# Weight splits on GpSimd in halves, one buffer more and other small moves in a hybrid decoder layer

## Chip, cores and metric

The kernel runs on one core of a Trainium2 chip. The metric is the device time of one execution in microseconds (us). A core has TensorE (PE in the profile; PEld is its loading of weights), VectorE (DVE), ScalarE (ACT), GpSimd (POOL) and SyncE (SP), which here only issues transfers.

## What is computed

One decoder layer in float32, with 512 tokens and a model width of 1024. A combined projection of the input feeds three token mixers; each is gated, projected back, gated again, and the merged result goes through an output projection and a LayerNorm.

```python
u = x @ w_in + b_in
a_x, a_z, b_q, b_k, b_v, b_z, i_q, i_k, i_w, c_q, c_kc, c_vc, c_ks, c_vs, c_kw, c_vw, c_g, c_z, g = split(u)
y_a = pool_mixer(a_x) * silu(a_z)
y_b = dsa_mixer(b_q, b_k, b_v, i_q, i_k, i_w) * silu(b_z)
y_c = nsa_mixer(c_q, c_kc, c_vc, c_ks, c_vs, c_kw, c_vw, c_g) * silu(c_z)
g = sigmoid(g)
m = g[0] * (y_a @ w_pa) + g[1] * (y_b @ w_pb) + g[2] * (y_c @ w_pc)
out = layernorm(ALPHA * x + m @ w_o)
```

The pool mixer takes trailing means over 2, 4, 8 and 16 tokens. The second mixer keeps the best keys of each query by an indexer's score. The third has a compressed, a selected and a window branch. The tests' inputs have larger spreads than usual for some weights; shapes are unchanged.

## The kernel before, in words

**Products in three parts.** Float32 accuracy comes from splitting each operand into a high and a low part: ScalarE rounds a copy into the high part (`h`), and the low part (`l`) is the original minus `h`. `mm3` (L67) then issues three matmuls of 512 columns: high by high, high by low and low by high (L68 to L70).

**Dense tiles.** The projection's weights are cut into 55 tiles of 128 outputs (128 x 1024 values, 512 KB). `dense` (L142) makes one tile in eight steps of three matmuls, into a PSUM buffer of the pool `pd` (three buffers) or `pq` (four). `load_w` (L87) brings a tile: a transfer into one of two staging buffers (`wst`), ScalarE's copy to `w_h` (L93), and the subtraction to `w_l` (L95). While `POOL[0]` is set, GpSimd issues the transfer and subtracts; at the start and the end SyncE and VectorE do. Smaller tiles of 512 columns (`wp`) serve the projections back (`branch_d`, L608).

**Opening.** Eight matmuls on a zeroed tile `idle` run while the first data come. `load_early` (L118) brings the first two weight tiles (numbers 0 and 3, `w0` and `w3`) in two halves each, `load_x` (L112) brings the input in eight pieces of 128 rows of the transpose (256 KB). The string in L129 gives their order: a and b are the first halves of the two weight tiles, c and d the second. L734 deals the steps of the first two dense tiles out in turns.

**Order of work.** TensorE's order is written out by hand: a stream `F` of generators (L742) is advanced a few steps between the pieces of the attention units (L809). The instructions of the other engines are placed by a planner from dependences, priorities and its own estimates of durations; instructions that are emitted under `high_priority` go ahead of others. Within an engine the order is then fixed.

**Attention units.** `Unit.front` (L423) makes scores (L443), adds a mask and takes the maximum on VectorE (L445), exponentials on ScalarE (L450), then the reciprocal and its scaling by a gate, `r` (L454 to L458), and probabilities `pc` or `pb` in two float16 parts: ScalarE L462, VectorE L464. The score's PSUM buffer is free after L464. `Compressed.probs` (L511) does the same for the compressed branch; its low part `cp` is made on VectorE in L524. Top-k rounds on VectorE (L305, L306) fill gaps.

**Small buffers.** The tag `b` has six buffers of 2 KB a partition. They hold gates (`z` in `silu2`, L403; `tg`), the pooling tiles (`x0`, the running sums `xs` that GpSimd adds in L569, and `za`), and a few constants. `silu2` reads a dense tile's PSUM twice on ScalarE, `tanh` (L407) and a biased copy into `z` (L153); then the PSUM buffer is free. `th`, `vc32` and `vc1` of the compression (L351, L384) are in another pool.

**Output projection.** `wo_mm` (L876) makes 512 x 512 in four row tiles for each half of the columns. For the first half the kernel takes seven of the eight steps of two tiles before the eighth of either (L891), because the last parts of the merged result (`mh`, `ml`) come late. `add_x` (L883) reads the PSUM on VectorE (L885) and frees it.

Of the kernel before, what the change touches and what calls it, by code (L numbers as in the profile page):

```python
# [7 lines left out]
F32 = mybir.dt.float32  # L8
F32R = mybir.dt.float32r
BF = mybir.dt.bfloat16  # L10
# [9 lines left out]
KT = D // 128  # L20
# [10 lines left out]
EARLY = (0, I_KK)  # L31
# [3 lines left out]
def trunk(ctx, tc, a, out, dbg=None):  # L35
    nc = tc.nc
# [4 lines left out]
    sp = ctx.enter_context(tc.tile_pool(name="sp", bufs=2))  # L41
# [1 line left out]
    pq = ctx.enter_context(tc.tile_pool(name="pq", bufs=4, space=PSUM))  # L43
    pv = ctx.enter_context(tc.tile_pool(name="pv", bufs=1, space=PSUM))

    BUFS = {"x": 8, "wst": 2, "wh": 3, "wl": 3, "s": 2, "p": 2, "pt": 2, "t": 16, "ks": 2, "b": 6}

    def big(tag, name, dt=F32, shape=(128, 2, 512)):
        return bp.tile(list(shape), dt, tag=tag, name=name, bufs=BUFS[tag])

    def sm(name, n=8, bufs=4):
        return sp.tile([128, n], F32, tag=name, name=name, bufs=bufs)

    def dps(name):
        return pd.tile([128, 512], F32, tag="pd", name=name)

    def qps(name):
        return pq.tile([128, 512], F32, tag="pq", name=name)

    def f(ap):  # L60
        return ap.bitcast(F32)

    def split(h, l, src):
        nc.scalar.activation(h, src, AF.Copy)
        nc.vector.tensor_sub(l, src, f(h))  # L65

    def mm3(ps, wh, wl, rh, rl, start, stop):  # L67
        nc.tensor.matmul(ps, wh, rh, start=start, stop=False)  # L68
        nc.tensor.matmul(ps, wh, rl, start=False, stop=False)  # L69
        nc.tensor.matmul(ps, wl, rh, start=False, stop=stop)  # L70
# [14 lines left out]
    POOL = [False]  # L85

    def load_w(src, n, tag="w"):  # L87
        st = big("wst", f"{tag}_st", F32, (128, 1024))[:, :n]
        h = big("wh", f"{tag}_h", F32R, (128, 1024))
        l = big("wl", f"{tag}_l", F32R, (128, 1024))  # L90
        with tc.high_priority():
            (nc.gpsimd if POOL[0] else nc.sync).dma_start(st, src)  # L92
            nc.scalar.activation(h[:, :n], st, AF.Copy)  # L93
            eng = nc.gpsimd if POOL[0] else nc.vector
            eng.tensor_sub(l[:, :n], st, f(h[:, :n]))  # L95
        return h, l


    idle = big("b", "idle", BF, (128, 512))
    nc.vector.memset(idle, 0.0)  # L100
    ps = qps("idle")
    for _ in range(8):
        nc.tensor.matmul(ps, idle[:, :128], idle, start=True, stop=True)


# [6 lines left out]
    def load_x(k):  # L112
        st = xst[k // 4][:, k % 4]
        dma = nc.sync.dma_start(st, a["xT"][:, k, :])
        split(xh[k // 2][:, k % 2, :], xl[k // 2][:, k % 2, :], st)
        return dma

    def load_early(i, c, n):  # L118
        if i not in early:
            early[i] = [big(t, f"w{i}{c}", d, (128, 1024)) for t, c, d in (  # L120
                ("s", "s", F32), ("t", "h", F32R), ("t", "l", F32R))]
        s = slice(c * 1024 // n, (c + 1) * 1024 // n)
        st, h, l = early[i]
        nc.sync.dma_start(st[:, s], a["wt"][i][:, s])
        split(h[:, s], l[:, s], st[:, s])

    bias = const("bias")
    with tc.high_priority():
        for k in "a01b23c4d567":  # L129
            if k in "abcd":  # L130
                load_early(EARLY["abcd".index(k) % 2], "abcd".index(k) // 2, 2)
            else:
                dma = load_x(int(k))
    ctx.enter_context(tc.issue_after(dma.ins))

    def X(part, k, s0=0, s1=S):
# [5 lines left out]
    def dense(i, s0=0, ps=None):  # L142
        wh, wl = early[i][1:] if i in early else load_w(a["wt"][i], 1024, f"w{i}")
        ps = (ps or dps)(f"d{i}")
        n = S - s0
        for k in range(KT):
            w = slice(k * 128, k * 128 + 128)
            mm3(ps[:, :n], wh[:, w], wl[:, w], X(0, k, s0), X(1, k, s0), k == 0, k == KT - 1)
            yield
        return ps[:, :n], bias[:, i:i + 1]  # L150
# [200 lines left out]
    def compress_mid(nm):  # L351
        w1h, w1l, bh, bl = CP[nm]
        ps = dps("cp" + nm)[:64, :62]
        for l in range(16):
            mm3(ps, w1h[:, l, :], w1l[:, l, :], bh[:, :, l], bl[:, :, l], l == 0, l == 15)
            if l % 4 == 3:
                yield
        th = sp.tile([64, 62], F32, name="th", bufs=1)
        nc.scalar.activation(th, ps, AF.Tanh, scale=0.5)
        z = big("b", "hz", F32, (64, 2, 4, 32))  # L360
        nc.vector.memset(z, 0.0)
        for g in range(2):
            c = slice(31 * g, 31 * g + 31)
            nc.vector.scalar_tensor_tensor(z[:, g, :, :31], th[:, None, c].to_broadcast([64, 4, 31]), 1.0,
                                           ps[:, None, c].to_broadcast([64, 4, 31]), op0=OP.add, op1=OP.mult)
        zh = big("b", "hth", F32R, (64, 2, 4, 32))
        zl = big("b", "htl", F32R, (64, 2, 4, 32))
        split(zh, zl, z)
        CP[nm] = zh, zl
# [13 lines left out]

    def compress_v():  # L384
        HH, HL, w2h, w2l = CP["v"] + W2[1]
        v32 = sp.tile([128, 2, 64], F32, name="vc32", bufs=1)
        ps = dps("vc")[:, :128].rearrange("p (g d) -> p g d", g=2)
        for g in range(2):
            mm3(ps[:, g], HH[:, g].rearrange("p r n -> p (r n)"), HL[:, g].rearrange("p r n -> p (r n)"),
                w2h, w2l, True, True)  # L390
        nc.vector.tensor_scalar(v32, ps, vscale, 0.5, op0=OP.mult, op1=OP.mult)
        for p in range(3):
            v1 = sp.tile([128, 2, 64], BF, name="vc1", bufs=2)
            nc.vector.tensor_copy(v1, v32)
            if p < 2:
                nc.vector.tensor_sub(v32, v32, v1)
            for h in range(4):
                r = slice(32 * h, 32 * h + 32)
                nc.gpsimd.tensor_copy(VC[p][r, :, h], v1[r])
        yield  # L400
# [207 lines left out]
    def branch_d(d, br, Y, t, dst):  # L608
        wh, wl = load_w(a["wp"][br, d], 512, f"wp{br}")
        ps = dps("pp")  # L610
        for e in range(4):
            w = slice(e * 128, e * 128 + 128)
            yh, yl = Y[e // 2]
            mm3(ps, wh[:, w], wl[:, w], yh[:, e % 2], yl[:, e % 2], e == 0, e == 3)
            yield
        with tc.high_priority():
            nc.vector.scalar_tensor_tensor(dst, t, 1.0, ps, op0=OP.add, op1=OP.mult)  # L617
# [113 lines left out]
    W2 = [compress_w2("k", 128), compress_w2("v", 64)]  # L731
    st = Stream([(dsa_keys,)])
    st2 = Stream([(f_kk, 0)])
    for n in (2, 1, 1, 1, 1, 1, 2):  # L734
        for _ in range(n):
            st.step()
        for _ in range(n):
            st2.step()
    Stream([(index_queries, 0), (f_qc, 0, 0), (values_load,), (index_queries, 1), (f_qc, 0, 1), (values,)]).rest()
    mcmp, rowv = small["mcmp"].rearrange("p (j n) -> p j n", j=NT), small["rowv"]  # L740
    POOL[0] = True
    F = Stream([(compress_in, I_KC, "k"), (vscales,), (compress_in, I_VC, "v"), (f_zc, 0, 0), (compress_mid, "k"),  # L742
                (f_zc, 0, 1), (compress_k,), (compress_mid, "v"), (f_qc, 1, 0), (f_qc, 1, 1), (compress_v,),
                (early_g, 0, 0), (f_kk, 1), (early_g, 0, 1), (f_pool,), (f_zc, 1, 0), (pool_x, 0), (early_g, 0, 2),
                (pool_z, 0), (pool_x, 1), (early_g, 0, 3), (pool_y, 0), (pool_z, 1), (pool_x, 2), (pool_y, 1),
# [130 lines left out]
    def wo_mm(ps, hf, t, k0, k1, c0=0, c1=512):  # L876
        c = slice(t * 128, (t + 1) * 128)
        for k in range(k0, k1):
            wh, wl = WO[hf][k // 2]
            mm3(ps[:, :c1 - c0], MH[k // 4][:, k % 4, c], ML[k // 2][:, k % 2, c], wh[:, k % 2, c0:c1],  # L880
                wl[:, k % 2, c0:c1], k == 0, k == KT - 1)

    def add_x(t, ps, c0, c1):  # L883
        z = Zt[t][:, c0:c1]
        nc.vector.scalar_tensor_tensor(z, ps[:, :c1 - c0], 0.5, z, op0=OP.mult, op1=OP.add)  # L885

    def stats(t, c0, c1):
        nc.vector.bn_stats(bst[t][:, c0 // 256 * 6:c0 // 256 * 6 + 6], Zt[t][:, c0:c1])

    bst = [sm("bst", 24) for _ in range(NT)]  # L890
    pss = [dps("wo"), dps("wo")]  # L891
    for k0, k1 in ((0, KT - 1), (KT - 1, KT)):
        for t in range(2):
            wo_mm(pss[t], 0, t, k0, k1)
    for t in range(NT):
        if t > 1:
            pss.append(dps("wo"))
            wo_mm(pss[t], 0, t, 0, KT)
        add_x(t, pss[t], 0, 512)
        for c in (0, 256):  # L900
            stats(t, c, c + 256)
    for t in range(NT):
# [17 lines left out]
        if not last:  # L920
            c = cs.pop()
# [81 lines left out]
```

## Time and profile before

| | |
|---|---|
| median of 3 runs | 529.67 us (529.11 to 530.96) |
| profiled execution | 529.6 us, of which the span from first to last instruction is 527.8 us |
| busy: TensorE, VectorE, ScalarE, GpSimd | 508.5, 378.7, 281.5, 219.8 us |
| mean granted TensorE clock | 0.991 of full speed |

The page gives busy time of each engine; matmuls are pipelined, so TensorE's busy time says that work is in flight and not that it runs at its peak. The list of waits says for which instruction of which engine an engine idled. A timeline row has the start, the duration, the engine, the line, the operation, output and inputs, and in brackets the engine's idle time just before and what ended it; "x2" means that two equal instructions in a row were merged.

### The profile page before, as it was taken

How to read it: one execution, taken by the hardware profiler on the slowest of the kernel's cores; microseconds unless marked ns; L12 is line 12 of the kernel's file. 1: busy time of each engine (PE TensorE's matmuls, PEld its weight loads, DVE VectorE, ACT ScalarE, POOL GpSimd, SP SyncE). 2: the span in 40 equal slices, each digit the busy share in tenths (PEclk: the TensorE clock that was granted, in tenths of full speed). 3: DMA queues.
4: the chain of work that ended last, by engine and by line, in shares of the span. 5: the costliest groups of instructions: out<-in, count | busy, mean ns of one | idle time of the engine just before them, and what ended most of it. 6: DMA issues, size and time to landing. Idle time of an engine off the chain costs nothing. (4 is left out here: it accounts for less than half of the span.)

```text
span 527.8 us, 7784 instructions
## 1 busy us (share of the span) xinstructions
PE 508.5 (96%) x2718; PEld 420.1 (80%) x2718; DVE 378.7 (72%) x912; ACT 281.5 (53%) x585; POOL 219.8 (42%) x205
## 2 busy tenths in 40 slices
PE   8999999988999999899999999999999999999993
PEld 5889878876888888688888788888788888887883
DVE  5773799789868798999787897956654345444276
ACT  6684475756566666673755647566663344432000
POOL 1424443463556467344544344427662112115042
PEclk9999999999999999899999999999999999999997
DMA  8622332168845342556534434453584445462012
GB/s 289 261 80 81 110 130 61 46 117 137 170 111 162 86 126 52 119 133 170 142 101 122 139 110 105 134 120 106 145 169 121 140 139 180 159 215 105 1 70 90
DMA packets 82135, 66.72 MB, mean 126 GB/s; under 512 B 67184, under 2 KB 68656, under 8 KB 82096
## 3 DMA queue, kind: packets, MB, share of 16 engines
q1 hardware_dynamic: 74912, 40.54, 28.9%
q0 software_dynamic: 7184, 25.69, 16.4%
q8 instruction: 21, 0.34, 0.3%
q14 instruction: 18, 0.15, 0.1%
HBM read 47.87 MB, written 2.10 MB: 95 GB/s over the span
## 5 line engine op out<-in xcount | busy, mean ns | idle before, releaser
L68 PE MATMUL d<-xh,w_h 128*128 128x512 f32 (+1 forms) x424 | 167.1, 394 | 2.6 <-ACT z L153 2.4
L69 PE MATMUL d<-xl,w_h 128*128 128x512 f32 (+1 forms) x424 | 165.2, 390 | 0.0
L70 PE MATMUL d<-xh,w_l 128*128 128x512 f32 (+1 forms) x424 | 165.1, 389 | 0.0
L95 POOL TENSOR_TENSOR w_l<-w_st,w_h 128x1024 fp32r<-128x1024 f32 x41 | 98.0, 2393 | 111.0 <-ACT w_h L93 109.9
L68 PEld LDWEIGHTS d<-xh,w_h 128*128 128x128 f32 x424 | 80.0, 189 | 18.5 <-ACT z L153 2.9
L70 PEld LDWEIGHTS d<-xh,w_l 128*128 128x128 f32 x424 | 79.9, 188 | 16.8
L69 PEld LDWEIGHTS d<-xl,w_h 128*128 128x128 f32 x424 | 79.9, 189 | 13.9
L93 ACT ACTIVATE w_h<-w_st 128x1024 fp32r<-128x1024 f32 x53 | 56.1, 1058 | 35.1 <-DMA w_st<-in_wt_dram 27.8
L450 ACT ACTIVATE qkc<-qkc,nb 128x512 f32<-128x512 f32 (+3 forms) x64 | 32.0, 500 | 51.2 <-DVE nb L445 32.5
L95 POOL TENSOR_TENSOR wp_l<-wp_st,wp_h 128x512 fp32r<-128x512 f32 x16 | 20.8, 1297 | 49.4 <-ACT wp_h L93 49.4
L464 DVE SCALAR_TENSOR_TENSOR pc<-qkc,r,pc 128x512 f16<-128x512 f32 (+3 forms) x64 | 32.7, 545 | 10.8 <-ACT pc L462 10.6
L643 POOL TENSOR_TENSOR m<-m,tg 128x512 f32<-128x512 f32 x12 | 16.5, 1377 | 52.8 <-DVE tg L617 52.6
L462 ACT ACTIVATE pc<-qkc,r 128x512 f16<-128x512 f32 (+3 forms) x64 | 29.8, 526 | 14.6 <-issue 7.1
L445 DVE CUSTOM_DVE_ANT_0 qkc<-qkc,cmask 128x512 f32<-128x512 f32 (+3 forms) x64 | 31.2, 495 | 2.7 <-PE qkc L443 2.3
L92 POOL DMA_DIRECT2D w_st<-in_wt_dram x41 | 23.3, 569 | 9.9 <-POOL w_l L95 5.3
L70 PE MATMUL wo<-woh,ml 128*128 128x512 f32 (+1 forms) x72 | 26.4, 367 | 0.4 <-DVE ml L65 0.4
L69 PE MATMUL wo<-wol,mh 128*128 128x512 f32 (+1 forms) x72 | 26.3, 366 | 0.0
L68 PE MATMUL wo<-woh,mh 128*128 128x512 f32 (+1 forms) x72 | 26.3, 366 | 0.0
L306 DVE MATCH_REPLACE8 acc<-m,acc 128x256 f32<-128x256 f32 (+2 forms) x48 | 26.0, 543 | 0.0
L95 DVE TENSOR_TENSOR w_l<-w_st,w_h 128x1024 fp32r<-128x1024 f32 x12 | 15.8, 1323 | 13.4 <-ACT w_h L93 13.4
L450 ACT ACTIVATE qkb<-qkb,nb 128x128 f32<-128x128 f32 (+3 forms) x32 | 16.0, 500 | 17.6 <-DVE nb L445 17.3
L305 DVE MAX8 m<-acc 128x8 f32<-128x256 f32 (+2 forms) x48 | 25.3, 549 | 0.0
(249 smaller groups left out, 1029.2 us busy)
## 6 DMA issues: line engine op xcount, KB each, us to landing
w_st<-in_wt_dram POOLq DMA_DIRECT2D x41, 512.0 KB, 3.8
w_st<-in_wt_dram SPq DMA_DIRECT2D x12, 512.0 KB, 3.8
wp_st<-in_wp_dram POOLq DMA_DIRECT2D x16, 256.0 KB, 3.0
wo_st<-in_wo_dram SPq DMA_DIRECT2D x8, 512.0 KB, 3.6
xst<-in_xT_dram SPq DMA_DIRECT2D x8, 256.0 KB, 4.7
wp_st<-in_wp_dram SPq DMA_DIRECT2D x8, 256.0 KB, 2.7
z<-in_x_dram SPq DMA_DIRECT2D x4, 512.0 KB, 5.0
wvst<-in_wve_dram SPq DMA_DIRECT2D x4, 320.0 KB, 7.1
```

Source lines behind the costliest of these rows:

```text
L68: nc.tensor.matmul(ps, wh, rh, start=start, stop=False)
L69: nc.tensor.matmul(ps, wh, rl, start=False, stop=False)
L70: nc.tensor.matmul(ps, wl, rh, start=False, stop=stop)
L92: (nc.gpsimd if POOL[0] else nc.sync).dma_start(st, src)
L93: nc.scalar.activation(h[:, :n], st, AF.Copy)
L95: eng.tensor_sub(l[:, :n], st, f(h[:, :n]))
L305: nc.vector.max(m8, negm[j])
L306: nc.vector.match_replace(negm[j], m8, negm[j], MARK)
L445: nc.vector.tensor_tensor_reduce(sc[i], sc[i], self.mask, -0.125, 3e38, OP.add, OP.min, nb[:, i:i + 1])
L450: nc.scalar.activation(sc[i], sc[i], AF.Exp, scale=-1.0, bias=nb[:, i:i + 1], accum_out=den[:, i:i + 1])
L462: nc.scalar.activation(p[:, 0, i], sc[i], AF.Copy, scale=r[:, i:i + 1])
L464: self.last = nc.vector.scalar_tensor_tensor(p[:, 1, i], sc[i], r[:, i:i + 1], p[:, 0, i], op0=OP.mult, op1=OP.subtract)
```

## The change

Seven small edits:

- `load_w` on GpSimd subtracts a tile in pieces of 512 columns: two instructions for a tile of 1024, one for a tile of 512 as before.
- The tag `b` has seven buffers in place of six, and `th`, `vc32` and `vc1` become tiles of that tag.
- Nine idle matmuls in place of eight.
- The two early weight tiles are loaded and split in quarters of 256 columns (128 KB), each ahead of one piece of the input.
- The steps of the first two dense tiles alternate singly.
- The output projection opens with three tiles in place of two.

```diff
-    BUFS = {"x": 8, "wst": 2, "wh": 3, "wl": 3, "s": 2, "p": 2, "pt": 2, "t": 16, "ks": 2, "b": 6}
+    BUFS = {"x": 8, "wst": 2, "wh": 3, "wl": 3, "s": 2, "p": 2, "pt": 2, "t": 16, "ks": 2, "b": 7}
...
             (nc.gpsimd if POOL[0] else nc.sync).dma_start(st, src)
             nc.scalar.activation(h[:, :n], st, AF.Copy)
-            eng = nc.gpsimd if POOL[0] else nc.vector
-            eng.tensor_sub(l[:, :n], st, f(h[:, :n]))
+            if POOL[0]:
+                for c in range(0, n, 512):
+                    nc.gpsimd.tensor_sub(l[:, c:c + 512], st[:, c:c + 512], f(h[:, c:c + 512]))
+            else:
+                nc.vector.tensor_sub(l[:, :n], st, f(h[:, :n]))
...
-    for _ in range(8):
+    for _ in range(9):
         nc.tensor.matmul(ps, idle[:, :128], idle, start=True, stop=True)
...
-        for k in "a01b23c4d567":
-            if k in "abcd":
-                load_early(EARLY["abcd".index(k) % 2], "abcd".index(k) // 2, 2)
-            else:
-                dma = load_x(int(k))
+        for k in range(KT):
+            load_early(EARLY[k % 2], k // 2, 4)
+            dma = load_x(k)
...
-        th = sp.tile([64, 62], F32, name="th", bufs=1)
+        th = big("b", "th", F32, (64, 62))
...
-        v32 = sp.tile([128, 2, 64], F32, name="vc32", bufs=1)
+        v32 = big("b", "vc32", F32, (128, 2, 64))
...
-            v1 = sp.tile([128, 2, 64], BF, name="vc1", bufs=2)
+            v1 = big("b", "vc1", BF, (128, 2, 64))
...
-    for n in (2, 1, 1, 1, 1, 1, 2):
+    for n in (1, 1, 1, 1, 1, 1, 1, 2):
...
-    pss = [dps("wo"), dps("wo")]
+    pss = [dps("wo") for _ in range(3)]
     for k0, k1 in ((0, KT - 1), (KT - 1, KT)):
-        for t in range(2):
+        for t in range(3):
             wo_mm(pss[t], 0, t, k0, k1)
     for t in range(NT):
-        if t > 1:
+        if t > 2:
             pss.append(dps("wo"))
             wo_mm(pss[t], 0, t, 0, KT)
```

## Rows read from the trace of the kernel before

**Rows 1.** The page: busy time of each engine; granted clock in 40 slices, in tenths.

```profile
PE 508.5 (96%) x2718; PEld 420.1 (80%) x2718; DVE 378.7 (72%) x912; ACT 281.5 (53%) x585; POOL 219.8 (42%) x205
...
PEclk9999999999999999899999999999999999999997
```

**Rows 2.** The waits of TensorE: total us, times, longest us.

```profile
PE qkc L443 <- DVE pc L464: 3.5, 3, 1.8
PE d L68 <- ACT z L153: 2.4, 1, 2.4
PE pp L68 <- DVE m L617: 1.2, 1, 1.2
```

**Rows 3.** Timeline of the opening, 0 to 17 us.

```profile
1.18 3.59 PE L103 MATMUL idle<-idle 128*128 128x512 bf16 x8 [1.18 <-DVE idle L100]
...
3.32 0.63 ACT L64 ACTIVATE w0h<-w0s 128x512 fp32r<-128x512 f32 x1 [1.32 <-DMA w0s<-in_wt_dram]
...
4.01 0.43 SPq L124 DMA_DIRECT2D w0s<-in_wt_dram  x1
...
5.05 0.63 ACT L64 ACTIVATE xh<-xst 128x512 fp32r<-128x512 f32 x1 [1.09 <-DMA xst<-in_xT_dram]
...
5.73 0.79 PE L68 MATMUL d<-xh,w0h 128*128 128x512 f32 x1 [0.95 <-ACT xh L64]
...
9.61 0.40 PE L70 MATMUL d<-xh,w3l 128*128 128x512 f32 x1
...
15.19 1.23 DVE L95 TENSOR_TENSOR w_l<-w_st,w_h 128x1024 fp32r<-128x1024 f32 x1 [1.45 <-ACT w_h L93]
```

**Rows 4.** Windows: length, PE, PEld, DVE, ACT, POOL busy; granted clock; DMA share; GB/s.

```profile
10.00:20.00 10.00, 10.00 (x48) 8.43 (x47) 7.19 (x10) 6.68 (x10) 0.21 (x1) 1.00 1.04 398
...
210.00:215.00 5.00, 2.56 (x11) 1.71 (x10) 3.31 (x8) 3.53 (x7) 2.55 (x6) 0.94 0.83 168
215.00:220.00 5.00, 5.00 (x18) 4.04 (x17) 5.00 (x13) 1.55 (x4) 1.52 (x2) 0.72 0.71 160
```

**Rows 5.** Timeline, 206 to 215 us.

```profile
206.79 2.38 POOL L95 TENSOR_TENSOR w_l<-w_st,w_h 128x1024 fp32r<-128x1024 f32 x1 [2.78 <-ACT w_h L93]
...
207.28 2.04 DVE L524 TENSOR_TENSOR cp<-cs,cp 128x128 f16<-128x128 f32 x1
...
209.14 1.07 POOL L569 TENSOR_TENSOR xs<-xs 128x508 f32<-128x508 f32 x1
...
214.14 0.60 PE L68 MATMUL d<-xh,w_h 128*128 128x512 f32 x1 [2.44 <-ACT z L153]
```

**Rows 6.** GpSimd's L95 by shape: busy us, mean ns; idle before. L458: shortest, median, longest ns.

```profile
L95 POOL TENSOR_TENSOR w_l<-w_st,w_h 128x1024 fp32r<-128x1024 f32 x41 | 98.0, 2393 | 111.0 <-ACT w_h L93 109.9 <-POOL vc L399 1.1
L95 POOL TENSOR_TENSOR wp_l<-wp_st,wp_h 128x512 fp32r<-128x512 f32 x16 | 20.8, 1297 | 49.4 <-ACT wp_h L93 49.4
...
L458 DVE TENSOR_TENSOR r<-r,gs x26: 150/165/2161, 100.9 to 301.0; 128x2 f32<-128x2 f32 x20, 128x4 f32<-128x4 f32 x6
```

**Rows 7.** Timeline, 124 to 128 us.

```profile
124.96 2.39 POOL L95 TENSOR_TENSOR w_l<-w_st,w_h 128x1024 fp32r<-128x1024 f32 x1 [0.62 <-ACT w_h L93]
125.20 2.16 DVE L458 TENSOR_TENSOR r<-r,gs 128x2 f32<-128x2 f32 x1
```

**Rows 8.** Timeline, 103 to 106 us.

```profile
103.72 2.32 DVE L396 TENSOR_TENSOR vc<-vc,vc 128x128 f32<-128x128 f32 x1
```

**Rows 9.** The chain that ended last, 273 to 293 us: start, us, what.

```profile
275.64 2.24 DVE cp L524
```

**Rows 10.** Timeline, 362 to 367 us: a subtraction on GpSimd and its first use.

```profile
362.65 2.40 POOL L95 TENSOR_TENSOR w_l<-w_st,w_h 128x1024 fp32r<-128x1024 f32 x1
...
366.89 0.40 PE L70 MATMUL d<-xh,w_l 128*128 128x512 f32 x1
```

**Rows 11.** Timeline of the output projection's start, 479 to 487 us.

```profile
479.36 0.50 PE L70 MATMUL wo<-woh,ml 128*128 128x512 f32 x1 [0.38 <-DVE ml L65]
...
485.36 0.69 DVE L885 SCALAR_TENSOR_TENSOR z<-wo,z 128x512 f32<-128x512 f32 x1 [3.24 <-PE wo L70]
```

## The prediction

> **What bounds the kernel now.** The page comes first: TensorE (PE) has matmuls in flight for 96% of the span, VectorE (DVE) is busy for 72% and GpSimd (POOL) for 42% [rows 1]. So only what keeps TensorE from issuing counts. Its list of waits [rows 2] is short: VectorE's `pc` 3.5 us in three waits, ScalarE's (ACT) `z` 2.4 in one, VectorE's `m` 1.2 in one, and smaller ones. They are not all that can be won. In the opening [rows 3] the idle matmuls begin at 1.18 and fill 3.59 us; the first real one starts at 5.73, behind the split of `xh`, and eight start by 9.61, 0.49 us apart (3.88/8). In the window from 10 to 20 us it is 48 in 10 us, 0.21 apart [rows 4]; a few of those are shorter. In mid-kernel the granted clock is full in all slices but one [rows 1]: it is 0.94 and 0.72 in two stretches of 5 us [rows 4], so 0.06*5 + 0.28*5 = 1.7 us of full speed are lost, right after the longest wait, the 2.44 us before the matmul at 214.14 [rows 5]. TensorE had idled that long, then ran at 1.2 GHz for a while, then at 2.4 again.
>
> Next I look at what stands behind the long waits. VectorE's scaling of `r` (L458) takes 0.15 us at best and 2.16 at worst [rows 6]. The long ones lie under GpSimd's weight subtraction (L95: 2.39 us for 1024 columns, 1.30 for 512 [rows 6]) and end with it. Near 129: L95 runs from 124.96 to 127.35, L458 starts at 125.20 and ends at 127.36, and two `pc` steps, for which TensorE waits, come after it [rows 7]. Near 113: L396, a subtraction of 128 columns, takes 2.32 us under another L95, and VectorE's queue behind it carries that on to a `pc` for which TensorE waits [rows 8]. Near 214: L95 runs from 206.79 to 209.17 and L524, as small, from 207.28 to 209.32; mask, `exp`, `r` and `pc` follow, and behind `pc` in ScalarE's queue stands `z`, whose end frees the PSUM buffer [rows 5]. The chain to the wait for `m`, at 292, goes back through VectorE and ScalarE alone to an L524 of 2.24 us [rows 9].
>
> **The change part by part.**
>
> *Halves on GpSimd.* Each of the 41 tiles of 1024 columns costs two times 1.30 in place of 2.39 [rows 6]: 0.21 us more, 8.6 us in all, on an engine that idles 58% of the span. The closest use that I found in GpSimd's stage: L95 ends at 365.05 and `w_l` is first read at 366.89 [rows 10], 1.8 us later. The second half ends 0.2 later than before, but is first read four steps on (12 matmuls, some 2.5 us), and the first half is ready 1.1 us earlier: cost 0. Without that cover TensorE would wait 0.2 per tile. The next transfer into the staging buffer goes out 0.2 later, under the same cover. The gain is a boundary in the middle at which VectorE can get through. That it gets through between two adjoining GpSimd instructions is in rows 5: the add of `xs` starts at 209.14 as L95 ends, and L524 ends at 209.32, long before that add. The instruction held up then ends up to 1.1 us sooner (2.39 - 1.30), and so do those queued behind it on VectorE, as long as VectorE doesn't idle. I take 1.0 at 113, 1.0 at 129, 1.0 at 214 and 0.9 at 292, bounds 0 and -3.9; the first two of the three waits for `pc` with 3.5, the others of waits of 2.4 and 1.2 [rows 2]. The wait at 214 shrinks to 1.4. Beside the waits for `pc`, of up to 1.8 [rows 2], the clock stays full [rows 1], so the loss of 1.7 goes too (bounds 0 and -1.7).
>
> *Opening.* Before, 256 KB of weights and 256 KB of `x` precede the first real matmul; after, 128 and 256. The splits of these two pieces start at 3.32 and 5.05 [rows 3], so 256 KB take 1.73 us here; later 398 GB/s flow [rows 4], 0.7 us for 256 KB. Half a piece saves 0.35 to 0.86; I take 0.5, nearer the steady rate because the 1.73 includes start-up. Nine idle matmuls at 3.59/8 = 0.45 each end near 5.2, where the first real one now comes, so the pause of 0.95 closes. Whether the clock is granted sooner no row shows. Eight real matmuls at 0.49 in place of 0.21 are 2.2 us, the splits of the first pieces among them: bounds 0 and -2.2, and I take -0.8, under the middle for those splits. SyncE issues 16 loads in place of 12; four more of 0.43 [rows 3] send the next weights out 1.7 us later. VectorE's split of those ends at 16.42 [rows 3]; the 40 matmuls after 9.61 last until 18.0 at 0.21, so 1.6 to spare, 0.3 if the opening gains 1.3. These data are issued long before they are split, so cost 0, at worst +1.4, the 1.7 less the 0.3. The steps taken singly in turn are the same 48 matmuls. Opening in sum: -1.3.
>
> The Trainium skill (DMA: Bandwidth & Descriptors, section Bandwidth, "Measured") speaks against small loads: 64 KB reach 138 GB/s and 1 MB 341, so it advises 1 MiB and more. By its figures a piece of 128 KB would cost nearly as much time as one of 256, and the 0.5 would be about 0. The 398 GB/s with loads of 256 and 512 KB in flight together [rows 4] don't agree with that, so the sum leaves it out.
>
> *Seven buffers, and `th`, `vc32`, `vc1` among them.* By the code `x0`, at most three sums, one `za` and the late `z` are in use from 206 to 214: six, so `z` may be late by its place in the queue alone. I take 0; if it was the buffer, the rest of that wait, 1.4, goes as well. `th`, `vc32` and `vc1` stand behind no wait in rows 2: 0. If they hold a buffer too long, the next `z` waits, as in the second rival.
>
> *Three tiles in the output projection.* The wait of 0.38 comes at tile 0, seventh step (479.36), for the split of `ml` [rows 11]: ahead of tile 1 in either kernel, so it stays. For the eighth step no wait is listed: nothing to win. New is that the fourth tile needs tile 0's buffer, freed by L885 (0.69 us [rows 11]) under six matmuls of 0.21: 0, at worst +0.7.
>
> *New order.* A planner places the instructions of ScalarE, VectorE and GpSimd, so every later wait can move. Bounds: 0, and one wait like that at 214 with its clock loss, 2.4 + 1.7 = +4.1. I take +1.4, about one wait like those at 113 and 292, since three of the four long waits were of that kind.
>
> Sum: -3.9 - 1.7 - 1.3 + 1.4 = -5.5, from the profiled execution's 529.6 (its span and 1.8 around it; 0.1 below the median of 529.67): 524.1.
>
> **Rivals.**
>
> *The halves give nothing* (0.10). GpSimd's second half follows at once and keeps VectorE out for both. For it: the halves adjoin in its queue. Against it: L524 at 209.32 [rows 5]. Only the opening is left: 528.3, inside what a measurement can't tell from no change.
>
> *One new long wait* (0.14). In the new order a ScalarE instruction that frees PSUM is late again, at 4.1. For it: at 214 it took only `z` behind `pc`. In place of the 1.4, the sum is -5.5 - 1.4 + 4.1 = -2.8, or 526.8; if the wait at 214 also stays whole (2.7 not won), 529.5, no change.
>
> *Slower* (0.15). The wait at 214 stays, and the pooling section (150 to 225), where the adds for `xs` share GpSimd's queue with twice as many weight instructions, gets two more such waits of 4.1 each: -1.3 - 2.9 + 8.2 = +4.0, or 533.6. It decides from the second new wait on; with one it is 529.5. Against it: GpSimd's busy share of 42%.
>
> **How the numbers follow.** My forecast has 0.61, the rivals 0.10, 0.14 and 0.15. A measurement of this kernel tells about 0.3%, 1.6 us, from no change, so the first rival and half of the second count as the same: faster 0.61 + 0.07 = 0.68, same 0.17, slower 0.15. The forecast alone spans 520.2 (-3.9 - 1.7 - 0.9 - 2.2, and half of the buffer's 1.4) to 527.6 (the opening's clock as before, +0.8, and the new wait at its upper bound, +2.7). The range takes in the first two rivals, the second up to 529.5 + 0.8 = 530.3, and leaves the slower one out: 520.2 to 530.3.
>
> **What would show it.** Right: L95 on GpSimd as 82 halves of 1.3 us; L458 and L524 at 1.5 us or less; full clock between 10 us and the end of the matmuls; the first real matmul near 5.2 and the fast spacing before 9.6; waits at `pc`, `z` and `m` below 4 us together. Wrong: L458 and L524 still above 2 us (first rival), or a new wait of 2.4 us or more with 1.2 GHz behind it.

## The result, and the profile after

The changed kernel takes **522.98 us** (median of 4 runs, 522.04 to 525.16) against 529.75 for the kernel before (4 runs, 529.11 to 530.96): a ratio of 0.988, interval 0.985 to 0.991. That is 6.4 us by the ratio; 524.1 was forecast. The profiled executions are 522.43 and 529.6 us, with spans of 520.7 and 527.8: 7.1 us apart. In a few executions a kernel took far longer, in most of them at a low mean granted clock (632.7 us at 0.754 for the halves alone); medians and ratios leave these out.

The page of the kernel after, against [rows 1, 6]. Most lines have a number one higher than before: L96 is the subtraction on GpSimd, L459 the scaling of `r`, L525 `cp`, L465 `pc`, L154 `z`, L618 `m`.

```profile
PE 506.6 (97%) x2719; PEld 418.5 (80%) x2719; DVE 364.8 (70%) x916; ACT 282.7 (54%) x589; POOL 229.5 (44%) x246
...
PEclk9999999999999999999999999999999999999998
...
L96 POOL TENSOR_TENSOR w_l<-w_st,w_h 128x512 fp32r<-128x512 f32 x82 | 107.7, 1332 | 106.6 <-ACT w_h L93 105.5
```

GpSimd is busy 9.7 us longer (82 halves, 107.7 us, for 41 tiles, 98.0), and VectorE 13.9 us less: what it lost was time in which an instruction was held up, not work. The slice with a lower clock is gone.

TensorE's waits after (total us, times, longest us), against [rows 2]:

```profile
PE wo L70 <- DVE ml L65: 1.1, 1, 1.1
PE d L68 <- ACT z L154: 1.1, 1, 1.1
PE cpk L69 <- DVE bkl L65: 1.1, 1, 1.1
PE qkc L444 <- DVE pc L465: 0.5, 1, 0.5
PE pool L68 <- ACT ph L64: 0.4, 1, 0.4
PE pool L69 <- DVE ph L65: 0.2, 1, 0.2
```

`pc`, `z` and `m` were 7.1 us together and are 1.6; `m` is gone from the list. `ml` and `bkl` have grown, and `ph` is new.

The timeline of the kernel after at the four places of [rows 5, 7, 8, 9], in order of time:

```profile
102.93 2.59 POOL L96 TENSOR_TENSOR w_l<-w_st,w_h 128x512 fp32r<-128x512 f32 x2 [0.60 <-POOL vc L400]
103.15 1.22 DVE L397 TENSOR_TENSOR vc<-vc,vc 128x128 f32<-128x128 f32 x1
...
122.54 0.14 DVE L459 TENSOR_TENSOR r<-r,gs 128x2 f32<-128x2 f32 x1
122.56 2.54 POOL L96 TENSOR_TENSOR w_l<-w_st,w_h 128x512 fp32r<-128x512 f32 x2 [0.89 <-ACT w_h L93]
...
203.11 2.57 POOL L96 TENSOR_TENSOR w_l<-w_st,w_h 128x512 fp32r<-128x512 f32 x2 [3.05 <-ACT w_h L93]
...
203.60 0.96 DVE L525 TENSOR_TENSOR cp<-cs,cp 128x128 f16<-128x128 f32 x1
...
208.80 0.50 PE L68 MATMUL d<-xh,w_h 128*128 128x512 f32 x1 [1.11 <-ACT z L154]
...
268.11 1.18 DVE L525 TENSOR_TENSOR cp<-cs,cp 128x128 f16<-128x128 f32 x1
...
285.28 0.50 PE L68 MATMUL pp<-yah,wp_h 128*128 128x512 f32 x1
```

L397 now ends at 104.37, half-way through the two halves that end at 105.52: 1.22 us in place of 2.32. L525 takes 0.96 in place of 2.04 and 1.18 in place of 2.24, and the `pp` matmul at 285.28 waits for nothing. At 122.54 the scaling of `r` is not held up at all: it comes 0.02 us ahead of the first half.

Where the 7.1 us come from is read by pairing the same matmul in both traces and subtracting the starts. The kernel after leads by 1.05 us at 28.9 us (times of before), and by 0.52 behind the wait for `bkl` at 71.5. Then the lead steps up by 1.04 at 113, 0.36 at 121, 2.03 at 129 and 1.41 at 214; by 1.43 more from 214 to 217.5, where the clock used to be low; down by 0.92 at 222 (`ph`); up by 1.34 to 292, of which 1.16 there, where the wait for `m` is gone; down by 0.84 at 479 (`ml`). The last matmul starts 6.34 us sooner, at 512.32 in place of 518.67, and the span ends another 0.82 us closer behind it.

These sizes are those of one execution each. Two kernels that differ from the one after only in the idle matmuls or in the tiles of the output projection (further down) step up by 1.3 and 1.2 at 129 and by 2.2 and 1.6 at 214, and the traces of kernels with the old opening lie from 2.8 us behind the kernel before to 1.2 ahead of it at 72 us.

The opening after, against [rows 3]:

```profile
1.19 4.02 PE L106 MATMUL idle<-idle 128*128 128x512 bf16 x9 [1.19 <-DVE idle L103]
...
4.23 0.63 ACT L64 ACTIVATE xh<-xst 128x512 fp32r<-128x512 f32 x1 [0.68 <-DMA xst<-in_xT_dram]
...
4.92 0.80 PE L68 MATMUL d<-xh,w0h 128*128 128x512 f32 x1
...
7.03 0.39 PE L69 MATMUL d<-xl,w3h 128*128 128x512 f32 x1
```

The pause of 0.95 us behind the idle matmuls is closed, the first real matmul is 0.81 us sooner, and from 7.03 on matmuls start 0.23 apart (9.61 before).

### The profile page after: what moved, and what is told of

It is laid out like the page before. It is cut to its first block, busy times and chain, and to the rows that moved or that the text cites. A ratio compares the mean times of both kernels' runs of the same rounds, so it can differ in the third digit from the quotient of the medians.

```text
span 520.7 us, 7843 instructions
## 1 busy us (share of the span) xinstructions
PE 506.6 (97%) x2719; PEld 418.5 (80%) x2719; DVE 364.8 (70%) x916; ACT 282.7 (54%) x589; POOL 229.5 (44%) x246
## 4 chain that ended last, share of the span: by engine, by line
PE 54%; DVE 3%; DMA 2%; ACT 1%; issue 0%; DVEq 0%; ACTq 0%
PE d L68 9%; PE d L69 9%; PE d L70 9%; PE pp L68 4%; PE pp L69 4%; PE pp L70 4%; PE acc L482 3%; PE wo L70 3%; PE wo L69 3%; PE wo L68 3%; PE qkb L444 2%; DMA wo_st<-in_wo_dram 2%; PE qkc L444 1%; DVE wol L65 1%; PE acc L533 1%; ACT woh L64 0%
## 5 line engine op out<-in xcount | busy, mean ns | idle before, releaser
L96 POOL TENSOR_TENSOR w_l<-w_st,w_h 128x512 fp32r<-128x512 f32 x82 | 107.7, 1332 | 106.6 <-ACT w_h L93 105.5
L465 DVE SCALAR_TENSOR_TENSOR pc<-qkc,r,pc 128x512 f16<-128x512 f32 (+3 forms) x64 | 32.6, 544 | 16.0 <-ACT pc L463 15.8
L96 POOL TENSOR_TENSOR wp_l<-wp_st,wp_h 128x512 fp32r<-128x512 f32 x16 | 20.6, 1286 | 41.8 <-ACT wp_h L93 41.7
L68 PE MATMUL pp<-yh,wp_h 128*128 128x512 f32 x64 | 25.1, 392 | 0.0
```

The costliest lines, as they stand in the source:

```text
L96: nc.gpsimd.tensor_sub(l[:, c:c + 512], st[:, c:c + 512], f(h[:, c:c + 512]))
L465: self.last = nc.vector.scalar_tensor_tensor(p[:, 1, i], sc[i], r[:, i:i + 1], p[:, 0, i], op0=OP.mult, op1=OP.subtract)
```

## The experiments

Ratios are to the kernel before, run on the same chip; two of the runs are single executions and have none.

**The halves alone, and all but the halves.** The first is the kernel before with this edit, the second the kernel after without it:

```diff
-            eng = nc.gpsimd if POOL[0] else nc.vector
-            eng.tensor_sub(l[:, :n], st, f(h[:, :n]))
+            if POOL[0]:
+                for c in range(0, n, 512):
+                    nc.gpsimd.tensor_sub(l[:, c:c + 512], st[:, c:c + 512], f(h[:, c:c + 512]))
+            else:
+                nc.vector.tensor_sub(l[:, :n], st, f(h[:, :n]))
```

> The kernel before with the halves on GpSimd alone. Theory (VectorE is held up by GpSimd's long subtraction, and a boundary in its middle lets it through): most of the gain, 523.5 to 525.5 us; L458 and L524 at 1.5 us or less in place of 2.2 and 2.5; the waits for pc near 129 and for m near 292 gone or under 0.5, the wait for z near 214 at 1.0 to 1.5 and no drop of the clock behind it; first real matmul at 5.7 as before. Rival A (the gain comes from the opening): 528.5 or more. Rival B (the gain comes from the seventh buffer, which frees z): the wait of 2.4 for z and the drop of the clock stay, 526 or more.

> The changed kernel with the subtraction on GpSimd whole again (2.4 us), all else as changed. Theory: 528.5 to 530, the instructions of over 2 us on VectorE are back, with waits for pc and z of 1.5 us and more. Rival A (opening): 524 to 525. Rival B (seventh buffer): no wait for z near 210, 524 to 526.

Halves alone: 524.89 us (three executions), ratio 0.9895 (0.986 to 0.993). All else: 529.07, ratio 0.997 (0.9954 to 0.9985). So the halves carry some 5.6 us of the 6.4, and without them the old waits are back. TensorE's waits in the kernel with all but the halves:

```profile
PE qkc L441 <- DVE pc L462: 3.3, 3, 1.6
PE d L68 <- ACT z L151: 2.6, 1, 2.6
...
PE pp L68 <- DVE m L615: 0.9, 1, 0.9
```

The timeline of the halves alone is read from one more execution:

> One more look at the kernel before with the halves alone. Theory: span 522.5 to 524 us; no instruction at L458 or L524 over 1.5 us; waits near 129 and 292 gone, those near 113 and 214 shrunk by 1 us each; first real matmul at 5.3 to 6.0 and a lead of 0.5 us or less at 71 us.

527.99 us in that one execution, with a span of 526.2, above the 522.5 to 524 expected. Its timeline shows why: in the opening TensorE paused 1.55 us for a split of `xh`, and then ran at half clock (0.63 us a matmul, 0.39 at full clock; granted 0.50 in the stretches from 8 to 14 us) until 14.5:

```profile
8.03 0.80 PE L68 MATMUL d<-xh,w0h 128*128 128x512 f32 x1 [1.55 <-ACT xh L64]
...
9.35 0.63 PE L70 MATMUL d<-xh,w0l 128*128 128x512 f32 x1
```

By the paired matmuls it is 2.8 us behind the kernel before at 12 us and 1.6 ahead at the last one: 4.3 us won in between, with the halves as the only edit.

**The opening alone.** Nine idle matmuls, quarters, single steps:

```diff
-    for _ in range(8):
+    for _ in range(9):
...
-        for k in "a01b23c4d567":
-            if k in "abcd":
-                load_early(EARLY["abcd".index(k) % 2], "abcd".index(k) // 2, 2)
-            else:
-                dma = load_x(int(k))
+        for k in range(KT):
+            load_early(EARLY[k % 2], k // 2, 4)
+            dma = load_x(k)
...
-    for n in (2, 1, 1, 1, 1, 1, 2):
+    for n in (1, 1, 1, 1, 1, 1, 1, 2):
```

> The kernel before with the new opening alone (nine idle matmuls, early weights in quarters, single steps). Theory: first real matmul near 4.9 and the fast spacing by about 7, 1.6 us ahead at 10 us, of which about 0.5 us is left at 71 us; 528.5 to 530 in all. Rival A: 524 to 525.5. If the lead is given back wholly to later waits: 529.7.

528.66 us, ratio 0.9969 (0.994 to 0.9996): about 1.6 us, with bounds of 0.2 and 3.1. The paired matmuls tell where: 2.16 us ahead at 9.85, 0.57 at 28.8, 0.48 at the last one. Most of the early lead runs into waits for `xh`, `xl` and `w_l` up to 28 us. Yet the span is 1.2 us shorter, because it ends 8.37 us behind its last matmul, where the kernel before ends 9.15 behind. (See the last experiment.)

**The buffers alone.**

```diff
-    BUFS = {"x": 8, "wst": 2, "wh": 3, "wl": 3, "s": 2, "p": 2, "pt": 2, "t": 16, "ks": 2, "b": 6}
+    BUFS = {"x": 8, "wst": 2, "wh": 3, "wl": 3, "s": 2, "p": 2, "pt": 2, "t": 16, "ks": 2, "b": 7}
...
-        th = sp.tile([64, 62], F32, name="th", bufs=1)
+        th = big("b", "th", F32, (64, 62))
...
-        v32 = sp.tile([128, 2, 64], F32, name="vc32", bufs=1)
+        v32 = big("b", "vc32", F32, (128, 2, 64))
...
-            v1 = sp.tile([128, 2, 64], BF, name="vc1", bufs=2)
+            v1 = big("b", "vc1", BF, (128, 2, 64))
```

> The kernel before with the seventh buffer of tag b alone (th, vc32 and vc1 moved into it as in the change). Theory: no change, 529.2 to 530.2, and the wait of 2.4 us for z near 214 with the drop of the clock is still there. Rival B: that wait is gone, and with it 2.5 to 4 us: 525.5 to 527.

530.19 us, ratio 0.999 (0.997 to 1.001). The wait at 214 stays, so `z` was late by its place in the queue, not for want of a buffer. From its list of waits:

```profile
PE d L68 <- ACT z L153: 2.5, 1, 2.5
```

**Two tiles at the start of the output projection; eight idle matmuls.** Each is the kernel after with one part put back:

```diff
-    pss = [dps("wo") for _ in range(3)]
+    pss = [dps("wo"), dps("wo")]
...
-        for t in range(3):
+        for t in range(2):
...
-        if t > 2:
+        if t > 1:
```

```diff
-    for _ in range(9):
+    for _ in range(8):
```

> The changed kernel with an output projection that opens with two tiles. Theory: the wait for ml at tile 0 is the same 1.1 us, no wait at the eighth step, no wait for tile 0's buffer in either; span within 0.3 us of the changed kernel from 470 us on. If the third tile helps: a new wait of 0.5 us or more for the last ml.

> The changed kernel with eight idle matmuls. Theory (closing the pause lets the granted clock rise during the opening and stay): a pause of 0.2 to 0.5 us before the first real matmul, the clock full by 6 to 10 us and in some executions later, a mean granted clock of 0.990 to 0.995 against 0.995; 523 to 524.5. If the ninth does nothing: clock as in the changed kernel, 523.0.

With two tiles: 523.48 us in one execution, inside the range of the kernel after, and the wait for `ml` is the same 1.1. With eight idle matmuls: 522.92, ratio 0.989 (0.985 to 0.993), as the kernel after. Neither of the two can be told from nothing.

**Which halves count.** Theory: the four tiles of [rows 5, 7, 8, 9], under which a small VectorE instruction is held up, give it all. They are the 9th, 12th, 23rd and 29th of the 41. One kernel halves only these, the other only the remaining 37 (`not in` for `in`):

```diff
+                count[0] += n == 1024
+                step = 512 if n == 1024 and count[0] in (9, 12, 23, 29) else n
+                for c in range(0, n, step):
+                    nc.gpsimd.tensor_sub(l[:, c:c + step], st[:, c:c + step], f(h[:, c:c + step]))
```

> The kernel before with only four of GpSimd's 41 subtractions in halves: those over the blocked instructions of VectorE at 103.7, 125.2, 207.3 and 275.6 us. Theory (four places where VectorE stands still and TensorE ends up waiting): nearly the whole gain of the halves, 524.5 to 526.5 us. Rival C (the gain is spread over all tiles, or comes from weights that are ready earlier): 529 to 530.

> The complement: the other 37 subtractions in halves, these four whole. Theory: 528.5 to 530, the four long waits of TensorE stay. Rival C: 525 to 526.

The four: 525.3 us, ratio 0.9908 (0.988 to 0.994). The others: 526.88, ratio 0.9939 (0.992 to 0.996). Four halved tiles do nearly what 41 do (0.9895), but the other 37 give 3.2 us as well, where none was expected, so the theory is too narrow. The two seem not to add up (4.9 + 3.2 for 5.6), though the times alone, each uncertain by 1 to 2 us, don't settle that. TensorE's waits, in the kernel with the four and then in that with the others:

```profile
PE qkc L448 <- DVE pc L469: 1.2, 3, 0.5
...
PE d L68 <- ACT z L158: 0.8, 1, 0.8
PE pp L68 <- DVE m L622: 0.7, 1, 0.7
```

```profile
PE d L68 <- ACT z L158: 2.3, 1, 2.3
PE qkc L448 <- DVE pc L469: 1.8, 2, 1.5
```

The wait at 214 hangs on its one tile: 0.8 and 2.3. Those at 129 and 292 do not. The timeline of the kernel with the others, where the tiles at 129 and before 292 are whole:

```profile
124.13 0.14 DVE L463 TENSOR_TENSOR r<-r,gs 128x2 f32<-128x2 f32 x1
126.21 2.39 POOL L98 TENSOR_TENSOR w_l<-w_st,w_h 128x1024 fp32r<-128x1024 f32 x1 [2.96 <-ACT w_h L93]
...
271.49 2.27 DVE L529 TENSOR_TENSOR cp<-cs,cp 128x128 f16<-128x128 f32 x1
...
288.66 0.51 PE L68 MATMUL pp<-yah,wp_h 128*128 128x512 f32 x1
```

Relieved at earlier tiles, VectorE reaches the scaling of `r` 2.1 us before that subtraction begins. So there are two ways out of one wait, to be let through half-way or to come first, and either takes much of the gain: 1.3 us at 129 with the four, 1.5 with the others, 2.0 with all. At 292 the prediction's culprit, the `cp` of [rows 9], still takes 2.27 us with the others, and the `pp` matmul waits for nothing; with the four it takes 1.21, and 0.7 of the wait stays. So that wait went by something that the other tiles moved, not by this `cp`; what it was is open.

**Smaller pieces.** The kernel after with 256 columns a piece:

```diff
-                for c in range(0, n, 512):
-                    nc.gpsimd.tensor_sub(l[:, c:c + 512], st[:, c:c + 512], f(h[:, c:c + 512]))
+                for c in range(0, n, 256):
+                    nc.gpsimd.tensor_sub(l[:, c:c + 256], st[:, c:c + 256], f(h[:, c:c + 256]))
```

> The changed kernel with GpSimd's subtractions in pieces of 256 columns (some 0.75 us each, 3.0 for a tile). Theory: VectorE is held up half as long again, but the waits left of which it is a cause are 1.1 (z near 209) and 0.5 (pc near 112), so 521.5 to 523; if GpSimd's extra 0.4 us a tile matters, the waits for w_l appear and it is 523.5 or more.

521.72 us, ratio 0.9844 (0.9825 to 0.9864): 1.3 us below the kernel after by the medians, though the intervals overlap. (The edit cuts the 16 tiles of 512 columns in two as well.) From its page and its list of waits:

```profile
L96 POOL TENSOR_TENSOR w_l<-w_st,w_h 128x256 fp32r<-128x256 f32 x164 | 120.8, 763 | 106.3 <-ACT w_h L93 102.0
```

```profile
PE acc L482 <- DMA ptb<-pb: 1.1, 1, 1.1
...
PE d L68 <- ACT z L154: 0.4, 1, 0.4
```

Four pieces cost 3.05 us in place of 2.39, 27 us more of GpSimd for the 41 tiles, and still TensorE waits for none of them. The waits for `pc` and `m` are gone and that for `z` is 0.4; a transfer (`ptb`) is late instead, 1.1 us at 392.

**GpSimd's other long instructions too.** The wait for `ml` looked like one more of the kind. The kernel after at the start of the output projection:

```profile
469.13 1.29 POOL L644 TENSOR_TENSOR m<-m,tg 128x512 f32<-128x512 f32 x1
...
469.37 2.13 DVE L65 TENSOR_TENSOR wol<-wo_st,woh 128x1024 fp32r<-128x1024 f32 x1 [0.64 <-ACT woh L64]
...
470.50 1.90 POOL L872 TENSOR_SCALAR z<-z 128x1024 f32<-128x1024 f32 x1
...
472.02 0.92 DVE L65 TENSOR_TENSOR ml<-m,mh 128x512 fp32r<-128x512 f32 x1
...
473.00 0.50 PE L70 MATMUL wo<-woh,ml 128*128 128x512 f32 x1 [1.12 <-DVE ml L65]
```

The split of `wol` takes 1.23 elsewhere and 2.13 here, under GpSimd's add to `m`; `tg` and `ml` queue behind it. In the kernel before the add ran from 475.48 to 476.77, and the split began as it ended:

```profile
476.53 1.32 DVE L65 TENSOR_TENSOR wol<-wo_st,woh 128x1024 fp32r<-128x1024 f32 x1 [2.02 <-ACT woh L64]
```

With the opening alone the split meets the add, and TensorE waits 1.1 us for `ml` there too, though it is only 1.4 us ahead of the kernel before:

```profile
475.24 2.14 DVE L65 TENSOR_TENSOR wol<-wo_st,woh 128x1024 fp32r<-128x1024 f32 x1 [0.63 <-ACT woh L64]
```

With four halved tiles TensorE is 4.9 us ahead, the split takes 1.32 and the wait is 0.4. So the wait goes with this meeting and not with how early TensorE comes: in all traces but that of the next experiment it is 0.9 to 1.1 where the split takes 2.1 us or more, and 0.4 to 0.6 where it takes 1.3. On top of quarters, then:

```diff
-            nc.gpsimd.tensor_add(m, m, t)
+            for c in (0, 256):
+                nc.gpsimd.tensor_add(m[:, c:c + 256], m[:, c:c + 256], t[:, c:c + 256])
...
-        nc.gpsimd.tensor_scalar(Zt[t], Zt[t], ALPHA, 1.0, op0=OP.mult, op1=OP.mult)
+        for c in range(0, 1024, 256):
+            nc.gpsimd.tensor_scalar(Zt[t][:, c:c + 256], Zt[t][:, c:c + 256], ALPHA, 1.0, op0=OP.mult, op1=OP.mult)
```

> The kernel with quarters, and two other long instructions of GpSimd in pieces of 256 columns: the sums m (1.28 us) and the scaling of z before the output projection (1.9 us). Theory: VectorE's split of the last wol, 2.1 us there for 1.2 at best, falls to 1.7 or less, and the wait for ml before the output projection from 1.1 to 0.5 or less; 520.5 to 521.5 us, faster than both kernels. If the wait for ml is set by the transfers of wo and not by GpSimd: the wait stays at 1.1, 521.7 as with quarters alone.

521.29 us (520.25 to 524.53), ratio 0.9851 (0.982 to 0.989): the same as quarters alone, where less was expected. The timeline is that of the longest of its six executions (524.53), in which TensorE also waits 2.0 us for `z`:

```profile
468.36 3.68 POOL L874 TENSOR_SCALAR z<-z 128x256 f32<-128x256 f32 x4 [7.82 <-DMA z<-in_x_dram]
...
470.55 1.22 DVE L65 TENSOR_TENSOR wol<-wo_st,woh 128x1024 fp32r<-128x1024 f32 x1 [0.62 <-ACT woh L64]
...
472.12 1.42 POOL L645 TENSOR_TENSOR m<-m,tg 128x256 f32<-128x256 f32 x2
...
474.26 0.50 PE L68 MATMUL wo<-woh,mh 128*128 128x512 f32 x1 [1.37 <-ACT mh L64]
```

`wol` is back to 1.22, but now the pieces on GpSimd are held up: the scaling of `z` takes 3.68 us with VectorE's work in between, where whole it takes 1.9. (Two of the four pieces take 1.24 and 1.41, each under a split of `wol`, the other two 0.4.) The add to `m` behind it starts at 472.12, and TensorE waits 1.4 us for `mh` where it had waited 1.1 for `ml`. The wait has moved.

**Why the span ends closer behind the last matmul.** Six kernels with the new opening, and the kernel after, end 8.33 to 8.37 us behind it; before and the four others with the old opening 9.10 to 9.16. VectorE's work there is the same. The new opening differs by four more loads on SyncE's queue. So the kernel before gets four idle loads:

```diff
     ctx.enter_context(tc.issue_after(dma.ins))
+    for i in range(4):
+        nc.sync.dma_start(cp.tile([128, 55], F32, name=f"bx{i}"), a["bias"])
```

> The kernel before, with four more loads on SyncE's queue right behind the opening: copies of the biases, 28 KB each, into tiles that nothing reads; the opening itself stays as before. Question: the kernels with the new opening end 8.3 to 8.4 us after their last matmul, those with the old one 9.1 to 9.2, and the new opening issues four loads more on that queue. Theory 'the number of transfers on the queue decides': 8.3 to 8.4 us from the last matmul to the end of the span, and some 0.8 us less in the time (ratio near 0.9985). Rival 'something else in the opening does it' (where its data lie, or which load stands where): 9.1 to 9.2 us and a ratio of 1.000. A start of the last matmul more than 1 us later than 518.7 would say that the four loads disturb the opening.

528.59 us, ratio 0.998 (0.996 to 1.001): in the time it can't be told from no change, but the trace is plain. Last matmul and last stores, in the kernel before, the one after, and the one with four loads (spans 527.8, 520.7, 526.8):

```profile
518.67 0.28 PE L70 MATMUL wo<-woh,ml 128*128 128x256 f32 x1
...
523.45 1.06 SPq L930 DMA_DIRECT2D out_dram<-z  x2
```

```profile
512.32 0.28 PE L70 MATMUL wo<-woh,ml 128*128 128x256 f32 x1
...
517.10 0.99 SPq L931 DMA_DIRECT2D out_dram<-z  x2
```

```profile
518.42 0.28 PE L70 MATMUL wo<-woh,ml 128*128 128x256 f32 x1
...
523.20 0.99 SPq L932 DMA_DIRECT2D out_dram<-z  x2
```

From the last matmul to the end: 9.15, 8.33 and 8.40 us. The last stores are issued 4.78 us behind the last matmul in all three, so the difference arises from there on. Four loads that nothing reads shorten the end by 0.75, so it goes with the four further issues on that queue, not with what the opening does with them.

## Why the prediction was right, and where its steps were not

The sum was -5.5 and the two profiled executions are 7.2 us apart; the time fell inside the forecast's own range. By steps:

- **Halves, -3.9 forecast: right in kind, too small.** The steps in the lead are 1.04 at 113 (1.0 forecast), 0.36 and 2.03 at 121 and 129 (1.0), 1.41 at 214 (1.0) and 1.16 at 292 (0.9): 6.0. A boundary in the middle gives at most half a tile, and that is what L397 and L525 show (1.10, 1.08 and 1.06 us less). At 129 it was more: with the earlier tiles halved VectorE came to the scaling of `r` before the subtraction began, and the whole wait went. (In the kernels with eight idle matmuls and with two tiles it came first too, and about 0.6 us of the wait stayed.) The step that failed here is the bound of 1.1 for each place: each was taken by itself, and relief at one tile moves the meeting at the next. At 292 the reading of the chain failed as well: the kernel with the others loses that wait with its `cp` still held up.
- **Cost of the halves on GpSimd, 0: right.** The tile of [rows 10] is ready at 356.16 and first read at 359.70: 3.5 us to spare, and no wait of TensorE in the list is for a `w_l` of L96.
- **That VectorE gets through between two adjoining GpSimd instructions: shown.** The first rival (0.10) falls with L397, L525 and the 0.9895 of the halves alone. This is as the Trainium skill has it (SBUF — State Buffer, section "SBUF: two separate sides"): GpSimd and VectorE share a port pair, and of a GpSimd instruction that reads SBUF and a VectorE instruction with two SBUF inputs the one that starts first holds it to its end and shuts the other out. The traces agree: L525 takes 0.96 under a piece of 1.29, where it took 2.04 under a whole tile, and the splitting of `z` shows the other side, a piece on GpSimd of 1.41 under VectorE's `wol`, where a free one takes 0.4.
- **Clock, -1.7 forecast: mis-sized.** The full clock between 214 and 217.5 does give 1.43 us, but 0.92 is lost at once to new waits at 222, since TensorE now reaches the pooling matmuls before `ph` is split:

```profile
215.84 0.51 PE L68 MATMUL pool<-ph,plhl 128*128 128x512 f32 x1 [0.38 <-ACT ph L64]
...
216.57 0.50 PE L69 MATMUL pool<-ph,plhl 128*128 128x512 f32 x1 [0.22 <-DVE ph L65]
```

  About 0.5 is left. A stretch at half clock had been covering for late work, which the step did not ask about. The other traces bear that out: with the buffers alone and with all but the halves the clock stayed full there, `z` was waited for as long as before, and the 0.4 and 0.2 for `ph` are there; in the four traces in which the clock fell they are not. That the loss goes because the wait shrinks is not shown: in six traces with a wait for `z` of 1.3 us or less the clock stayed full, but so it did in three with 2.3 to 2.6 (last section).
- **Opening, -1.3 forecast: right in sum, not in make-up.** 0.5 us is left of it at 71 us and 0.8 comes at the end of the kernel, with the four further loads on the queue, where nothing was forecast. One pair of traces says little about that 0.5: other traces of the old opening differ by more. The first real matmul was to come near 5.2 and came at 4.92, with the split of `xh` 0.8 sooner in this pair, at the upper bound of the 0.35 to 0.86; by the medians of six traces with the old opening (4.83) and seven with the new (4.35) it is 0.5, as forecast. The prediction's other reading, that by the figures of the Trainium skill (DMA: Bandwidth & Descriptors, section Bandwidth, "Measured") half the piece would bring about 0, was wrong: a straight line between that table's 0.95 us for 64 KB and 6.15 for 1 MB gives, as an estimate, 1.3 us for 128 KB and 2.0 for 256, so 0.7 saved. The 0.5 measured here is nearer to that than to 0.
- **Seven buffers, 0, and three tiles, 0: right** as far as the runs can tell (0.999; with two tiles the same wait for `ml`, in one execution).
- **New order, +1.4 forecast: the step that failed.** The planner hardly changed the order: 895 of the 912 VectorE instructions before and 576 of ScalarE's 585 stand in the same sequence after. No wait of 2.4 us came. What came are small losses: `ph` 0.6, where TensorE runs into work that had time before; `ml` 0.7 more, from the meeting of `wol` with GpSimd's add, which came with the opening alone too; and `bkl` 0.6 more, whose cause is open. The second and the third rival both needed a new wait of 4.1 and had nothing like it.

So -3.9, -1.7, -1.3 and +1.4 stand against about -6.0, -0.5, -1.3 and +0.8, with 0.2 in steps too small to place: in all 7.2. The halves gave 2.1 more than forecast, the clock 1.2 less and the new order cost 0.6 less, and the sum came out 1.7 short by the profiled executions, 1.1 by the medians. That it is so near is in part luck, since the errors of the halves and of the clock offset each other.

Each mark of the last part of the prediction is there: 82 halves at 1.33, L459 at most 1.02 and L525 at most 1.41 us, full clock from 10 us to the end of the matmuls, fast spacing from 7.03, and 1.6 us of waits for `pc`, `z` and `m`.

## What to carry to other kernels

When a short VectorE instruction takes as long as the GpSimd instruction beside it and ends with it, cut the GpSimd instruction into pieces: the cost is on an engine with time to spare (44% busy here), and here halves alone gave 1.05%. Quarters in the whole change reached 521.72 us, below the 522.98 of the halves by the medians, so they are the version to take, though the intervals overlap. Cut what stands in VectorE's way, not what TensorE waits for, since the pieces themselves can be held up. Price a stall by what comes next: ask which work will be late once TensorE arrives sooner, and whether two stalls share one gain.

## What the runs showed that was not expected

**The end of the kernel goes with how many transfers went through SyncE's queue before**: four more, and the span ends 0.75 us sooner behind the last matmul (9.15 against 8.40). Why is open; other numbers than four were not tried.

**The clock does not follow the length of the wait alone.** TensorE's wait for `z`, the granted clock in the two stretches of 5 us in which it ends and TensorE goes on (205 to 215 us with all pieces, 210 to 220 in the others), and the time at full speed that this costs:

| kernel | wait, us | granted clock | lost, us |
|---|---|---|---|
| before | 2.44 | 0.94, 0.72 | 1.7 |
| opening alone | 2.44 | 0.90, 0.76 | 1.7 |
| four loads | 2.40 | 0.81, 0.85 | 1.7 |
| all pieces | 2.02 | 0.93, 0.73 | 1.7 |
| all but the halves | 2.57 | 1.00, 1.00 | 0 |
| buffers alone | 2.45 | 1.00, 1.00 | 0 |
| the others (37) | 2.28 | 1.00, 1.00 | 0 |

The window behind the wait in the kernel with all but the halves (columns as in [rows 4]), to be read against the 0.72 there:

```profile
215.00:220.00 5.00, 5.00 (x24) 4.10 (x23) 5.00 (x14) 1.55 (x4) 1.70 (x2) 1.00 0.66 172
```

After much the same pause TensorE went on at 2.4 GHz in three kernels and at 1.2 for a while in four, one execution of each. Where the clock fell, it cost the same 1.7 us, but it did not fall behind every such wait. So a clock loss seen behind one wait, in one profile, is not a fixed price of that wait, and the prediction was wrong to take it as one.
